# Twelve weight remainders of the first mixer on VectorE instead of in an accumulating DMA, and another order of taking buffers in the second mixer

## The chip, the cores and the metric

The kernel runs on one core of a Trainium2 chip. The metric is the device time of one execution in microseconds (us). All numbers below come from three timed runs of the kernel before and from one profiled execution of it.

## The reference

Two decoder layers over 256 tokens of width 1024 in float32, then a final RMSNorm. Cut to what matters:

```python
x = x + gdn_shortconv_mixer(rms_norm(x), ...)   # layer 0: (256,1024) @ (1024,3600), conv, delta rule, @ (1024,1024)
x = x + squared_relu_mlp(rms_norm(x), ...)      # (256,1024) @ (1024,4096), relu^2, @ (4096,1024)
x = x + nsa_mixer(rms_norm(x), ...)             # layer 1: projections, sparse attention, @ (1024,1024)
x = x + squared_relu_mlp(rms_norm(x), ...)
return rms_norm(x, final_norm)
```

The delta rule of layer 0 works in two chunks per head group: scores of keys against keys, the inverse of a unit lower triangular matrix, then products with values, state and queries. In the kernel the inverse is a ladder of products of 32x32 blocks, in which each step needs the one before it.

## The kernel before, in words

**Weights.** All weights are read once, in pieces of 128 x 1024 float32 (512 KB; the first two pieces of the first layer are smaller, and the compressing weights of layer 1 are used as they are). SyncE's queue issues the loads in order into 8 stage buffers `st`; a load waits until its buffer has been let go (flag `st{slot}`). A piece (a "unit", 204 of them, numbered from 0) isn't used as float32: it is split into a rounded part `uh`, in the type float32r, and the remainder `ul` = `st` - `uh`. A product takes three matmuls: `uh` with the activation's rounded part, `uh` with the activation's remainder, `ul` with the activation's rounded part (`mm256`). A unit of 1024 columns has 8 blocks of 128, so 24 matmuls.

**Who makes the parts.** Two streams run through the units, one through the even numbers and one through the odd (`splits(0)`, `splits(1)`, lines 941 and 942). ScalarE copies `st` into `uh`. There are two ways to `ul`. Normally VectorE subtracts (line 531). For the units that `BYDMA` (line 37) lists, ScalarE first writes -`uh` into `ul`, and then GpSimd issues a DMA that adds `st` onto it (`refill`, line 534). There are four buffers each of `uh` and `ul`; a unit's buffers come free when TensorE has read the unit (flag `ud{i}`). A stage buffer is let go when its unit's `ul` is there (`split_done`), with either way. Units 16 to 35 are projections of the first mixer (four units each for values, queries, and the three parts of the short convolution), 36 to 43 its output projection, 44 to 107 the first MLP, 108 to 139 the second mixer, 140 to 203 the second MLP.

**Who sets the order.** The program is a set of Python generators ("streams"). A planner (`Order`, `run`) holds an estimate of each engine's free time and each instruction's cost, and always lets the stream go on that can start first; ties go to the lower priority number. The order on each engine is fixed in that way when the kernel is built, and on the chip each engine runs its list in order. A stream asks for an engine (`yield 'V'`), for a PSUM bank (`yield BANK`; there are eight), for a flag, or for a token (`yield 'take', name, count`, given back by `give`). The chain of the delta rule has priority 0, the splits 0.5, most else 1 or more; the main stream, which issues the projections, comes last in ties, and fills TensorE between the steps of the chain.

**The chain of the first mixer.** `chain_k` norms the keys, `prepare` forms the key scores `al` and their transposes, `invert` runs the ladder (`tt`, `ys`, `uc` on VectorE, 128 matmuls of 32x32 per step on TensorE), `chain_main` solves for the values, `output` makes `o` and then `ya`, the input of the last four units of the output projection (40 to 43). The query convolution and the short convolution run on GpSimd (`pool_conv`: `tap`, `cvpool`, `CG`).

**The second mixer.** For each of eight head pairs, `attend` makes scores and exponentials `PX`, `weigh` scales them, `combine` spawns four `turn` streams, each of which transposes three 128 x 128 blocks of `PX` on TensorE into a PSUM bank and copies them into one of four buffers `pts`; `products` multiplies them with the values and gives the four `pts` tokens back.

Line 329 is that of a helper that records every compute instruction, so nearly all rows of the profile name it; tiles tell the instructions apart.

Of the kernel before, what the change touches and what calls it, by code (L numbers as in the profile page):

```python
# [33 lines left out]
KPOOL, VPOOL, QPOOL, CVB = (), (), (0, 1, 2, 3), {'conv': 4, 'pool': 2}  # L34
TAP = {'V': 290}
CHAIN, EARLY, TOK_FIRST = 0, 16, False
BYDMA, DLAT = (*range(20, 44, 2), *range(113, 121, 2), *range(129, 141, 2)), 4500
YIELD = (0.0, 0.0, 0.0)
TICK, BUSY = 10240 / 3, 1500.0
FULL, DRAIN, BARE, STAY, LEAVE = (128, 128), 0.0, 0.0, 0.0, 0.0  # L40
# [125 lines left out]
class Order:  # L166
# [21 lines left out]
    def spawn(self, gen, prio=None):  # L188
        c = self.cur
        if prio is None:  # L190
            prio = 1 if c is None or c.prio in (MAIN, SPLIT) else c.prio
        s = Stream(gen, prio, c)
        self.streams.append(s)
        self._next(s, None)

    def flag(self, name):
        self.flags.setdefault(name, self._now())
# [5 lines left out]
    def release(self, bank):  # L203
        self.banks.append((self._now(), self.held.pop(id(bank))[0]))

    def give(self, name):
        self.tokens[name].append(self._now())
# [178 lines left out]
SLOTS, PTS = 4, 4  # L386
# [1179 lines left out]
def layer1(e, n, nxt):  # L1566
# [3 lines left out]
    spawn, flag, release, give = order.spawn, order.flag, order.release, order.give  # L1570
    with ExitStack() as ctx:
# [44 lines left out]
        def copy(dst, src, eng):  # L1616
            n = int(np.prod(src.shape[1:]))
            ps = src.space == PSUM
            pick = yield dict(A=(52 if ps else 95) + 0.83 * n, V=68 + (1.04 if ps else 0.52) * n) if PK else eng
            if pick == 'A':  # L1620
                A.activation(dst, src, AF.Copy)
            else:
                V.tensor_copy(dst, src)
# [157 lines left out]
        def attend(i, p, QQ, use):  # L1781
# [55 lines left out]
            give('qr')  # L1837
            spawn(weigh(i, p, PX, den))
            spawn(combine(i, p, PX))

        def soften(u, s, t, bank, sc, PX, nm, den):
# [98 lines left out]
        def combine(i, p, PX):  # L1940
            u = 2 * i + p
            yield 'flag', f'pw{u}.0'
            if not MERGE:
                ob = yield BANK
                O = ob[:, :T]
            turns, spreads, ts4 = [4], [2], {}
            for b in range(2):
                yield 'flag', f'pw{u}.{b}'
                tss = ts4[b] = [None, None]
                for s in range(2):  # L1950
                    spawn(turn(u, b, s, PX, tss, turns), TURN)
                if not MERGE:
                    spawn(spread(i, p, b, tss, O, spreads))
            if MERGE:
                for b in range(2):
                    for s in range(2):
                        yield 'flag', f'ts{u}.{b}{s}'
                ob = yield BANK
                O = ob[:, :T]
                yield SMALL  # L1960
                for b in range(2):
                    products(p, b, ts4[b], O, not b)
            else:
                yield 'flag', f'pv{u}'
            yield 'flag', 'cmp1'
            yield 'flag', f'pct{i}'
            yield 'PE'
            pct, left = pcts[i]
            if CL:
                x = pct.rearrange("p a t q -> p a (t q)")  # L1970
                e.mm256(O, *VCB2[p], x[:, 0], x[:, 1], False, True)
            else:
                PE.matmul(O, VCB2[p], pct.rearrange("p t q -> p (t q)"), start=False, stop=True)
            left[0] -= 1
            if not left[0]:
                give('pct')
            if ohl[i] is None:
                ohl[i] = p1.tile([128, 2, 2, T], F32R, name=f"ohl{i}", tag=f"ohl{i}")
            yield from hilo(ohl[i][:, 0, p], ohl[i][:, 1, p], O)
            release(ob)  # L1980
            flag(f'o{u}')

        def turn(u, b, s, PX, tss, left):
            tb = yield BANK
            tp = tb[:, :384]
            yield 'take', 'pts', PTS
            yield 'PE'
            e.keep(tb)
            PE.transpose(tp[:, :128], PX[0][:, s, b], ident)
            PE.transpose(tp[:, 128:256], PX[1][:, s, b, :128], ident)  # L1990
            PE.transpose(tp[:, 256:], PX[1][:, s, b, 128:], ident)
            left[0] -= 1
            if not left[0]:
                give(f'slot{u % SLOTS}')
            ts = p2.tile([128, 384], F32, name="pts", tag="pts", bufs=PTS)
            yield from copy(ts, tp, 'V' if s else 'A')
            release(tb)
            tss[s] = ts
            flag(f'ts{u}.{b}{s}')

        def products(p, b, tss, O, first):
            for s in range(2):
                g = 2 * p + s
                PE.matmul(O[64 * s:64 * s + 64], VT[:, 0, b, g * 64:g * 64 + 64], tss[s][:, :256],
                          start=first, stop=False)
            for s in range(2):
                g = 2 * p + s
                PE.matmul(O[64 * s:64 * s + 64, 128:], VT[:, 1, b, g * 64:g * 64 + 64], tss[s][:, 256:],
                          start=False, stop=False)
                give('pts')  # L2010

        def spread(i, p, b, tss, O, left):
            for s in range(2):
                yield 'flag', f'ts{2 * i + p}.{b}{s}'
            yield SMALL
            products(p, b, tss, O, left[0] == 2)
            left[0] -= 1
            if not left[0]:
                flag(f'pv{2 * i + p}')
# [63 lines left out]
```

## Time and profile before

| | |
|---|---|
| three timed runs | 672.41, 672.96, 673.91 us (median 672.96) |
| the profiled execution | 674.54 us, of which the span from first to last instruction is 672.7 us |
| TensorE (PE) | busy 97% of the span, weight loads (PEld) 93%, granted clock 0.988 on the mean |
| VectorE (DVE), ScalarE (ACT), GpSimd (POOL) | busy 68%, 58%, 20% |
| weight loads by SyncE's queue | 107.66 MB, 49.1% of 16 DMA engines' time |
| GpSimd's queue (the accumulating DMAs) | 11.54 MB, 9.0%, 22 issues of 512 KB, 5.4 us from issue to landing |
| instruction fetches (queue q8) | 52 packets of together 0.85 MB |

TensorE is busy nearly all the time, so the table alone doesn't tell what a change in one stage is worth: the stretches, the waits and the granted clock have to be read stage by stage. Times in rows are microseconds from the first instruction; a clock of 1.00 is 2.4 GHz and 0.50 is 1.2 GHz.

### The profile page before, as it was taken

How to read it: one execution, taken by the hardware profiler on the slowest of the kernel's cores; microseconds unless marked ns; L12 is line 12 of the kernel's file. 1: busy time of each engine (PE TensorE's matmuls, PEld its weight loads, DVE VectorE, ACT ScalarE, POOL GpSimd, SP SyncE). 2: the span in 40 equal slices, each digit the busy share in tenths (PEclk: the TensorE clock that was granted, in tenths of full speed). 3: DMA queues.
4: the chain of work that ended last, by engine and by line, in shares of the span. 5: the costliest groups of instructions: out<-in, count | busy, mean ns of one | idle time of the engine just before them, and what ended most of it. 6: DMA issues, size and time to landing. Idle time of an engine off the chain costs nothing.

```text
span 672.7 us, 16231 instructions
## 1 busy us (share of the span) xinstructions
PE 650.2 (97%) x6642; PEld 623.5 (93%) x6644; DVE 460.4 (68%) x899; ACT 387.7 (58%) x727; POOL 134.4 (20%) x179
## 2 busy tenths in 40 slices
PE   8999789999999999999999999999999999999995
PEld 5999679988999999999999886898999999999995
DVE  6998445865887776555566898897678777644441
ACT  7577234445676665434446679898567666434430
POOL 1012765611300000012024352120220000012121
PEclk9999789999999999999999999999999999999999
DMA  8884654556666666666666748653555555555401
GB/s 293 301 211 157 174 147 120 140 150 154 222 186 190 193 192 196 198 193 190 193 189 160 223 158 291 185 128 89 170 206 188 189 195 200 197 191 189 158 1 63
DMA packets 35642, 120.62 MB, mean 179 GB/s; under 512 B 4080, under 2 KB 4592, under 8 KB 35568
## 3 DMA queue, kind: packets, MB, share of 16 engines
q1 hardware_dynamic: 32112, 107.66, 49.1%
q0 software_dynamic: 3168, 11.54, 9.0%
q8 instruction: 52, 0.85, 0.5%
q10 hardware_dynamic: 288, 0.39, 0.2%
q14 instruction: 22, 0.18, 0.1%
HBM read 106.99 MB, written 1.05 MB: 161 GB/s over the span
## 4 chain that ended last, share of the span: by engine, by line
PE 80%; DVE 9%; ACT 4%; issue 3%; DMA 2%; SPq 0%; DVEq 0%; ACTq 0%
PE b L329 80%; DVE ul L329 2%; ACT uh L329 1%; DMA ul<-st 1%; DMA X<-xt 1%; DMA st<-wts 1%; DVE cvconv L329 1%; DVE rqt L329 1%; ACT E L329 1%; ACT ul L329 1%; DVE al L329 1%; DVE lc L329 0%; DVE u L329 0%; DVE tt L329 0%; DVE nacc L329 0%
## 5 line engine op out<-in xcount | busy, mean ns | idle before, releaser
L329 ACT ACTIVATE uh<-st 128x1024 fp32r<-128x1024 f32 (+3 forms) x204 | 206.2, 1012 | 218.4 <-PE b L329 187.5
L329 PE MATMUL b<-x,uh 128*128 128x256 f32 x1664 | 295.6, 282 | 2.0 <-ACT uh L329 1.8
L329 DVE TENSOR_TENSOR ul<-st,uh 128x1024 fp32r<-128x1024 f32 (+3 forms) x182 | 213.9, 1177 | 119.2 <-ACT uh L329 118.9
L329 PEld LDWEIGHTS b<-x,uh 128*128 128x128 f32 x1664 | 254.2, 190 | 4.1 <-ACT uh L329 1.7
L329 PE MATMUL b<-x,ul 128*128 128x256 f32 x832 | 233.1, 280 | 2.5 <-DVE ul L329 1.3
L329 PE MATMUL b<-U,uh 128*128 128x256 f32 x1024 | 174.2, 276 | 0.0
L329 PEld LDWEIGHTS b<-x,ul 128*128 128x128 f32 x832 | 158.2, 190 | 4.0 <-DVE ul L329 2.6
L329 PEld LDWEIGHTS b<-U,uh 128*128 128x128 f32 x1024 | 154.1, 188 | 0.0
L329 PE MATMUL b<-U,ul 128*128 128x256 f32 x512 | 141.3, 276 | 0.0
L329 PEld LDWEIGHTS b<-U,ul 128*128 128x128 f32 x512 | 96.1, 188 | 0.0
L329 POOL TENSOR_TENSOR nacc<-nacc,sq 128x256 f32<-128x256 f32 x24 | 32.4, 1348 | 227.1 <-ACT sq L329 217.4
L329 POOL DMA_DIRECT2D ul<-st x22 | 19.3, 876 | 80.4 <-ACT ul L329 36.4
L329 DVE SCALAR_TENSOR_TENSOR t<-b,rbc 128x256 f32<-128x256 f32 x64 | 26.6, 424 | 8.3 <-PE b L329 8.3
L329 ACT ACTIVATE U<-u 128x256 fp32r<-128x256 f32 x64 | 26.8, 419 | 2.0
L329 ACT ACTIVATE px<-b,nm 128x256 f32<-128x256 f32 (+1 forms) x64 | 26.3, 423 | 2.0 <-DVE nm L329 1.7
L329 DVE TENSOR_TENSOR U<-u,U 128x256 fp32r<-128x256 f32 x64 | 26.5, 419 | 0.0
L329 POOL TENSOR_TENSOR X<-X,par 128x256 f32<-128x256 f32 x8 | 5.6, 702 | 100.3 <-ACT nacc L329 91.7
L329 ACT ACTIVATE u<-t 128x256 f32<-128x256 f32 x64 | 25.6, 401 | 0.0
L329 DVE TENSOR_TENSOR X<-X,b 128x256 f32<-128x256 f32 (+1 forms) x28 | 13.9, 514 | 16.1 <-PE b L329 16.1
L329 PE MATMUL b<-uh,x 128*128 128x264 f32 (+1 forms) x128 | 24.5, 288 | 0.0
L329 PE MATMUL b<-ohl,uh 128*128 128x256 f32 x128 | 23.9, 287 | 0.2
L329 ACT ACTIVATE ul<-uh 128x1024 fp32r<-128x1024 f32 x22 | 23.2, 1057 | 0.4
(276 smaller groups left out, 793.9 us busy)
## 6 DMA issues: line engine op xcount, KB each, us to landing
st<-wts SPq DMA_DIRECT2D x188, 512.0 KB, 4.3
ul<-st POOLq DMA_DIRECT2D x22, 512.0 KB, 5.4
st<-wts SPq DMA_DIRECT2D x8, 280.0 KB, 3.2
st<-wts SPq DMA_DIRECT2D x8, 264.0 KB, 5.9
st<-wts SPq DMA_DIRECT2D x8, 256.0 KB, 6.1
X<-xt SPq DMA_DIRECT2D x3, 256.0 KB, 6.1
par<-par SPq DMA_DIRECT2D x1, 525.0 KB, 5.8
out_dram<-X SPq DMA_DIRECT2D x2, 256.0 KB, 2.7
```

Source lines behind the costliest of these rows:

```text
L329: r = f(*a, **k)
```

## The change

`BYDMA` loses the twelve even units from 20 to 42. Their remainders are made by VectorE's subtraction; ScalarE's writing of -`uh`, GpSimd's DMA issue and the transfer go away for them. The ten units of the second mixer in the list (113 to 119 and 129 to 139, every second one) stay.

In `combine`, the stream of a head pair first takes a token `turns`, of which there is one; it comes back when all four `turn` streams of that pair have taken their `pts` token. And a `turn` takes its `pts` token ahead of its PSUM bank, not after it. The number of buffers, banks and instructions in the second mixer is as before.

```diff
-BYDMA, DLAT = (*range(20, 44, 2), *range(113, 121, 2), *range(129, 141, 2)), 4500
+BYDMA, DLAT = (*range(113, 121, 2), *range(129, 141, 2)), 4500
...
-            turns, spreads, ts4 = [4], [2], {}
+            turns, spreads, ts4 = [4, 4], [2], {}
+            yield 'take', 'turns', 1
...
         def turn(u, b, s, PX, tss, left):
+            yield 'take', 'pts', PTS
+            left[1] -= 1
+            if not left[1]:
+                give('turns')
             tb = yield BANK
             tp = tb[:, :384]
-            yield 'take', 'pts', PTS
             yield 'PE'
             e.keep(tb)
```

## Rows read from the trace of the kernel before

**Rows 1.** Busy time by stretch. Columns: stretch, its length, then busy us (and instructions) of TensorE, of its weight loads, of VectorE, ScalarE and GpSimd, then granted clock, busy share of the DMA engines and GB/s.

```profile
60.00:80.00 20.00, 15.64 (x356) 15.12 (x355) 13.77 (x31) 7.12 (x7) 10.36 (x14) 0.90 0.64 162
80.00:100.00 20.00, 17.08 (x588) 16.00 (x587) 9.41 (x19) 7.51 (x12) 13.69 (x19) 0.84 0.52 129
100.00:120.00 20.00, 20.00 (x485) 19.27 (x485) 11.63 (x29) 8.04 (x12) 11.03 (x17) 0.92 0.45 121
220.00:260.00 40.00, 40.00 (x356) 40.00 (x355) 29.24 (x45) 26.02 (x44) 0.00 (x0) 1.00 0.65 194
```

**Rows 2.** What TensorE waited for from 20 to 190 us: us in total, times, the longest. "issue" is time in which it waited for nothing that the profile shows.

```profile
PE b L329 <- issue: 5.9, 3, 4.1
PE b L329 <- ACT uh L329: 1.1, 1, 1.1
```

**Rows 3.** The timeline of TensorE: the four matmul groups that began after these waits (start, length, instructions, idle time before them).

```profile
76.72 0.49 PE L329 MATMUL b<-ys,uc 32*32 32x32 f32 x21 [4.10 <-issue]
...
86.44 0.34 PE L329 MATMUL b<-ys,uc 32*32 32x32 f32 x18 [0.35 <-issue]
...
94.89 1.25 PE L329 MATMUL b<-ys,uc 32*32 32x32 f32 x122 [1.49 <-issue]
...
98.61 0.37 PE L329 MATMUL b<-x,uh 128*128 128x256 f32 x1 [1.08 <-ACT uh L329]
```

**Rows 4.** DMA packets by queue (packets, MB, share of 16 engines) in four short stretches: 74.3 to 74.5, 83.8 to 84.1, 92.5 to 92.9 and 96.0 to 96.5 us. q8 carries instructions, q0 GpSimd's DMAs, q1 the weight loads; the rows of q8 are shown in that order, after the two data queues of the longer stretch from 62.6 to 74.3 us, in which q8 has no packet.

```profile
q0 software_dynamic: 258, 0.99, 42.7%
q1 hardware_dynamic: 289, 1.05, 34.4%
...
q8 instruction: 1, 0.02, 29.7%
...
q8 instruction: 1, 0.02, 26.3%
...
q8 instruction: 1, 0.02, 15.8%
...
q8 instruction: 1, 0.02, 14.9%
```

**Rows 5.** As rows 4, the data queues from 90 to 98.6 us.

```profile
q0 software_dynamic: 144, 0.52, 31.6%
q1 hardware_dynamic: 201, 0.69, 26.6%
```

**Rows 6.** Stretches cut at the waits and at the changes of the granted clock, columns as in rows 1.

```profile
57.00:72.60 15.60, 15.34 (x317) 14.54 (x317) 14.79 (x38) 6.96 (x8) 5.70 (x7) 1.00 0.57 144
72.60:76.70 4.10, 0.02 (x3) 0.00 (x0) 0.81 (x2) 0.00 (x0) 3.86 (x7) 0.89 0.81 223
76.70:83.00 6.30, 6.28 (x181) 6.00 (x183) 1.38 (x4) 2.42 (x3) 3.43 (x5) 0.53 0.36 98
96.00:103.00 7.00, 5.92 (x43) 5.79 (x30) 2.89 (x6) 2.28 (x5) 0.00 (x0) 0.52 0.50 149
104.00:124.00 20.00, 19.86 (x517) 18.84 (x515) 15.48 (x40) 8.53 (x12) 14.79 (x23) 1.00 0.46 110
```

**Rows 7.** What SyncE's queue, which issues the weight loads, waited for most from 20 to 190 us.

```profile
SPq L482 <- DMA ul<-st: 88.1, 12, 11.4
```

**Rows 8.** Groups of instructions from 36 to 174 us: engine, operation, tiles, count, busy us, mean ns, idle time before.

```profile
L329 DVE TENSOR_TENSOR ul<-st,uh 128x1024 fp32r<-128x1024 f32 x16 | 20.2, 1266 | 9.1 <-ACT uh L329 9.1
L329 ACT ACTIVATE ul<-uh 128x1024 fp32r<-128x1024 f32 x12 | 12.7, 1059 | 0.4
L329 POOL DMA_DIRECT2D ul<-st x12 | 10.6, 880 | 43.8 <-ACT lsq L329 20.6 <-ACT ul L329 14.6 <-ACT eg L329 5.8
```

**Rows 9.** The timelines of ScalarE and VectorE: first the two writings of -`uh` between 57 and 72.6 us, then the step `ys` of the chain's ladder.

```profile
60.82 1.06 ACT L329 ACTIVATE ul<-uh 128x1024 fp32r<-128x1024 f32 x1
...
66.26 1.06 ACT L329 ACTIVATE ul<-uh 128x1024 fp32r<-128x1024 f32 x1
...
69.84 1.52 DVE L329 TENSOR_TENSOR ul<-st,uh 128x1024 fp32r<-128x1024 f32 x1
71.28 0.74 DVE L329 TENSOR_TENSOR ys<-b,par 128x256 f32<-128x256 f32 x2
```

**Rows 10.** The chain's end: ScalarE's timeline, and the last waits of TensorE ahead of `ya`'s matmuls.

```profile
152.71 1.06 ACT L329 ACTIVATE ul<-uh 128x1024 fp32r<-128x1024 f32 x1
153.67 0.61 ACT L329 ACTIVATE osq<-o 128x512 f32<-128x512 f32 x1
...
161.42 0.38 PE L329 MATMUL b<-ya,uh 128*128 128x256 f32 x1 [0.69 <-ACT ya L329]
...
162.15 0.39 PE L329 MATMUL b<-ya,uh 128*128 128x256 f32 x1 [0.34 <-DVE ya L329]
```

**Rows 11.** GpSimd and VectorE side by side: a convolution step of GpSimd alone, a subtraction of VectorE, and the same step of GpSimd while that subtraction ran.

```profile
83.72 0.61 POOL L329 TENSOR_TENSOR cvpool<-prepool,par 128x256 f32<-128x256 f32 x1
...
85.93 1.43 DVE L329 TENSOR_TENSOR ul<-st,uh 128x1024 fp32r<-128x1024 f32 x1 [0.57 <-ACT uh L329]
86.23 1.60 POOL L329 TENSOR_TENSOR cvpool<-prepool,par 128x256 f32<-128x256 f32 x1
```

**Rows 12.** The attention of the second mixer: a stretch as in rows 1, and the largest wait of TensorE from 360 to 490 us.

```profile
400.00:420.00 20.00, 19.59 (x166) 13.13 (x165) 17.27 (x45) 18.07 (x58) 6.70 (x13) 1.00 0.74 239
...
PE b L329 <- DMA ul<-st: 1.1, 1, 1.1
```

## The prediction, made before the result was known

> **What bounds the kernel now.** I read the stretches first. In the MLP TensorE is busy in every microsecond at full clock, 356 matmuls in 40 us [rows 1]; there an edit of VectorE's or a DMA's work buys nothing. The first mixer is where the change works (units 20 to 42, from about 38 to 160 us), and it has the one weak stretch of the kernel: from 60 to 100 us TensorE is idle for 4.36 + 2.92 us, and from 60 to 120 us its granted clock is 0.84 to 0.92 on the mean [rows 1]. So I read the waits of that part. The largest isn't for an engine: 5.9 us of "issue" in three waits, then 1.1 us put down to ScalarE's `uh` [rows 2]. The timeline places them: 4.10, 0.35, 1.49 and 1.08 us, together 7.02 us, three of them in the middle of a group of 32x32 matmuls [rows 3].
>
> What released them is seen in the DMA queues. Just ahead of each of the four, the instruction queue q8 moved one 16 KB packet (first seen in the stretches from 74.3, 83.8, 92.5 and 96.0 us), and TensorE went on 2.4 to 2.6 us after the start of those stretches. Before the longest wait no such packet had moved from 62.6 to 74.3 us, while GpSimd's queue took 42.7% and the weight loads 34.4% of the sixteen engines [rows 4]. I read this as: the ladder's short matmuls use up instructions faster than anywhere else (317 matmuls from 57 to 72.6 us [rows 6] against 356 in 40 us), TensorE runs out of them, and the next packet is late because data transfers are ahead of it. That also covers the fourth wait, since the `uh` it is put down to ended only because TensorE itself had come late.
>
> The clock follows the gaps: 0.53 from 76.7 to 83 us, after the longest, and 0.52 from 96 to 103 us, after the third [rows 6]; both are stretches at 1.2 GHz but for their edges. From 104 to 124 us there are as many short matmuls, TensorE is busy for 19.86 of 20 us, and the clock is 1.00 [rows 6]: the ladder alone doesn't lower it.
>
> The Trainium skill says otherwise of the first point ("Runtime: NRT & Kernel Launch", section "Instruction fetch mechanics"): instructions are refilled in blocks of 16 KiB over a DMA queue of their own, and crossing a block costs little because it is mostly hidden. The packet size agrees with rows 4, the hiding doesn't in these four places. What the kernel would do if the waits weren't due to the refill is a rival below.
>
> **The change, part by part.** The sum is made against the profiled execution, 674.54 us (span 672.7 us and 1.84 us around it); the median of the runs shown is 1.58 us lower, and the forecast is moved by that.
>
> *Transfers that go away.* Twelve accumulating transfers of 512 KB leave. In the worst stretch they were 42.7 of 77.1 parts of the traffic (55%), from 90 to 98.6 us 31.6 of 58.2 (54%) [rows 4, 5]. They also bunch the weight loads: SyncE's queue waits 88.1 us in twelve waits for these transfers before it may refill a stage buffer [rows 7], and the odd unit behind is then ready too, so two loads go out back to back. With VectorE's subtraction the buffers come free one by one. I scale each wait by the traffic left: 4.10 x 0.45 = 1.8, 1.49 and 1.08 x 0.46 = 1.2, and 0.35 to 0, since only q0 was busy in that spot. 3.0 us stay, 4.0 us go. Bounds: 0 and 7.0 us.
>
> *Clock.* The two slow stretches cost half their TensorE work: 6.28 x (1 - 0.53) = 3.0 us and 5.92 x (1 - 0.52) = 2.8 us, together 5.8 us. Without the long gap I expect no first drop; the second is less sure, since two shorter gaps made it. I take 4.5 us; bounds 0 and 5.8 us.
>
> *VectorE.* Twelve subtractions come in; sixteen in the same stretch took 1.266 us each [rows 8], so 12 x 1.266 = 15.2 us of work. ScalarE loses 12 x 1.059 = 12.7 us, GpSimd 12 x 0.88 = 10.6 us [rows 8]. VectorE's work lies beside TensorE's where the chain isn't late, so only what delays the chain counts. From 57 to 72.6 us VectorE is busy for 14.79 of 15.60 us and carries the chain into the ladder [rows 6]; two of the units fall there (their -`uh` at 60.82 and 66.26 us), and how such a subtraction sits in front of a step is seen at 69.84 us, where `ys` follows at once [rows 9]. That is 2 x 1.266 = 2.5 us in full. The other ten meet a VectorE that is idle about 30 to 50% of the time [rows 1]; a chain step comes every few microseconds, and I take a fifteenth part of each as delay, 10 x 1.266 / 15 = 0.8 us, an estimate. At the end the chain gains: `osq` starts right behind a writing of -`uh` (152.71 to 153.67 us), so it can start 1.0 us earlier, but a subtraction comes in on VectorE in the same place; I count 0.3 us of gain. Sum: 3.0 us later. It counts in full, because the chain's end is already what TensorE waits for: 0.69 + 0.34 us ahead of `ya`'s matmuls [rows 10]. Bounds: -1.0 us (only `osq`'s gain) and 15.2 us (all twelve on the chain).
>
> What is queued behind the new subtraction: on VectorE the chain's steps and the evacuations of banks. The subtraction itself waits for ScalarE's `uh`, as VectorE's sixteen do now, for 9.1 us in all [rows 8]; twelve more of these waits are in the 3.0 us as far as they hit the chain.
>
> *GpSimd.* Its in-order list loses the waits for -`uh`, 14.6 us [rows 8], and the issues. I cost this at nothing, since TensorE's list of waits doesn't name GpSimd; bounds -1 and 1 us. The Trainium skill has a rule against the change here ("SBUF — State Buffer", the part on the port pair that VectorE and GpSimd share): a VectorE operation with two SBUF inputs and a GpSimd operation that reads SBUF shut each other out for the whole instruction. The trace agrees: a convolution step of 0.61 us takes 1.60 us beside a subtraction [rows 11]. By the rule each new subtraction that meets one costs GpSimd 1.0 us, about what the lost issue gives back, so the sum stays.
>
> *Second mixer.* TensorE is idle for 0.41 of 20 us from 400 to 420 us, and its largest wait there is 1.1 us for an accumulating transfer that stays [rows 12]. Taking `pts` ahead of the bank frees banks for scores, and the token `turns` can hold back the next head pair's transposes, which would wait for `pts` anyway. I take 0; bounds -1 and 2 us, a shift of the planner's order included.
>
> Sum: -4.0 - 4.5 + 3.0 = -5.5 us, so 669.0 us for a profiled execution and 667.5 us for the median. The likeliest case's own range is 663 to 671 us.
>
> **The rivals.** *All gaps go, the clock stays up and the chain is hidden:* -7.0 - 5.8 = -12.8 us, 660.2 us. For it: the bunched loads go with the transfers. Against: weight loads alone still hold up refills. *It evens out:* the waits shrink by 4.0 us, both slow stretches stay, the chain costs 3.0 us: 672.0 us; for it, the ladder's short matmuls stay what they are. *VectorE becomes the bound (slower):* the place is the run from 57 us through the ladder to the solves at 104 to 124 us, where VectorE is busy for 15.48 of 20 us [rows 6]; the price is 1.266 us for every subtraction that stands ahead of a chain step. It decides from the seventh on, where 7 x 1.266 = 8.9 us exceeds the 8.5 us of gain; with nine, 672.96 - 8.5 + 11.4 = 675.9 us. For it: both ends of the chain are without slack. Against: the planner lets the chain go first in a tie. *The gaps have another cause and stay:* only the 3.0 us count, 676.0 us; this is what the skill's rule on refills amounts to. Against it stand the four packets. *The change doesn't do what it says* can only hold for its second part (0 us, in the sum already).
>
> **How the numbers follow.** Forecast 0.50, everything hidden 0.13, evens out 0.15, VectorE the bound 0.12, another cause 0.10. A difference under 0.2% (1.35 us) can't be told from no change for this kernel, so "same" is 671.6 to 674.3 us. Of the forecast 0.48 lies below, 0.02 within; of "evens out" 0.05 below and 0.10 within; all of the first rival is faster, and nearly all of the last two slower. Faster 0.66, same 0.13, slower 0.21. The range must reach to both sides: 661 us leaves out about half of the first rival, 675.5 us a bit over half of the last two.
>
> **What would show it.** Right: no packet on q0 before about 360 us; no gap of over 2 us on "issue" between 55 and 105 us and at most one stretch at 1.2 GHz there; SyncE's queue no longer waiting for `ul<-st`; the matmuls on `ya` beginning some 5 us before 161.4 us, with TensorE's wait ahead of them longer than 1.0 us by the chain's delay. Wrong: the same gaps at the same q8 packets without q0 in the way (then weights alone starve the refill), a wait for `ya` of 6 us or more (VectorE bound), or a difference that arises after 360 us.

## The result and the profile after

The changed kernel takes 666.62 us (median of four runs, 665.16 to 667.17); the kernel before, run beside it on the same chip, takes 673.43 us. The medians differ by 6.8 us. The ratio estimated from the single runs is 0.9883, with a 95% interval of 0.9845 to 0.9922, so by the ratio it is 7.9 us (5.2 to 10.4). 667.5 us had been forecast. The profiled execution took 666.40 us with a span of 664.6 us, 8.1 us shorter than before; the accounts below are made against that.

Where the span became shorter is read from the times at which the same matmuls start on TensorE in both traces (us; the last column is worked out from unrounded times):

| TensorE | before | after | difference |
|---|---|---|---|
| first matmul of the ladder (`tt,al`) | 68.57 | 68.53 | 0.0 |
| last matmul of the ladder (`ys,uc`) | 120.47 | 111.01 | -9.5 |
| first matmul on `ya` | 161.42 | 154.25 | -7.2 |
| last matmul on `ya`,`uh` | 172.84 | 164.90 | -7.9 |
| last matmul of the first MLP on `U`,`uh` | 348.6 | 340.6 | -7.9 |
| first matmul of the second MLP on `U`,`uh` | 575.5 | 567.0 | -8.5 |

The gain is made in one place, the ladder, which takes 42.5 us where it took 51.9. Not all of these 9.5 us are saved, for 26 fewer matmuls lie in it (the ladder from its first matmul to its last, before and after, columns as in [rows 1]):

```profile
68.57:120.66 52.09, 44.81 (x1376) 42.55 (x1375) 27.17 (x62) 17.36 (x25) 34.00 (x49) 0.87 0.56 147
...
68.53:111.20 42.67, 39.09 (x1350) 36.84 (x1349) 33.02 (x65) 11.89 (x20) 34.03 (x44) 0.96 0.37 112
```

From there to the first matmul on `ya` it is 2.3 us more than before. Of these, 2.0 us are work that came over from the ladder (447 matmuls in 41.15 busy us, where there were 425 in 39.16), and 0.3 us are waits. `ya`'s own matmuls bring 0.8 us, and the rest of the kernel runs as before to within 0.6 us.

The stretches answer to [rows 1, 6], columns as there:

```profile
60.00:80.00 20.00, 18.90 (x513) 18.29 (x513) 18.72 (x37) 4.85 (x6) 7.83 (x11) 1.00 0.51 161
80.00:100.00 20.00, 17.52 (x595) 16.05 (x594) 13.04 (x23) 5.69 (x9) 18.39 (x24) 0.91 0.31 87
100.00:120.00 20.00, 19.07 (x419) 18.09 (x418) 17.40 (x42) 7.01 (x13) 12.19 (x18) 1.00 0.32 101
...
90.00:93.00 3.00, 1.22 (x53) 1.06 (x41) 1.27 (x4) 0.42 (x1) 2.77 (x6) 1.00 0.63 182
93.00:96.80 3.80, 3.80 (x98) 3.58 (x100) 2.23 (x6) 1.23 (x2) 2.89 (x5) 0.55 0.03 10
```

From 60 to 80 us TensorE now does 513 matmuls where it did 356, at full clock. One short stretch at 1.2 GHz is left (0.55 from 93.0 to 96.8 us, its edges included), where there were two [rows 6]. It too stands right behind a gap: from 90 to 93 us TensorE is busy for 1.22 us only.

TensorE's waits from 20 to 190 us, and the two groups that began after "issue", answer to [rows 2, 3]:

```profile
PE b L329 <- issue: 2.2, 2, 1.8
PE b L329 <- DVE ys L329: 1.4, 2, 1.1
PE b L329 <- DVE u L329: 0.9, 2, 0.7
PE b L329 <- DVE yb L329: 0.6, 1, 0.6
```

```profile
88.46 0.39 PE L329 MATMUL b<-x,ul 128*128 128x256 f32 x1 [0.43 <-issue]
...
92.19 0.25 PE L329 MATMUL b<-ys,uc 32*32 32x32 f32 x4 [1.78 <-issue]
```

The four waits of together 7.0 us have become two of 2.2 us. In their place stand small waits for VectorE, 2.9 us in all, of which hardly any were there before (the rows of before that [rows 2] doesn't show):

```profile
PE b L329 <- DVE o L329: 0.7, 2, 0.4
PE b L329 <- ACT ya L329: 0.7, 1, 0.7
PE b L329 <- ACT Vf L329: 0.7, 1, 0.7
...
PE b L329 <- DVE ya L329: 0.3, 1, 0.3
PE b L329 <- DVE ys L329: 0.3, 1, 0.3
```

Just ahead of the wait of 1.78 us the DMA queues from 89.0 to 90.3 us show what moved beside the instruction packet; this answers to [rows 4]:

```profile
q1 hardware_dynamic: 108, 0.39, 73.8%
q8 instruction: 1, 0.02, 5.0%
```

GpSimd's queue is empty here, and the weight loads alone fill 73.8% of the sixteen engines. That they are what keeps this wait isn't shown: e5 below has the same wait almost without loads.

SyncE's queue has a new first wait, which answers to [rows 7]; the subtractions of the same stretch answer to [rows 8]:

```profile
SPq L482 <- DVE ul L329: 58.2, 22, 7.7
```

```profile
L329 DVE TENSOR_TENSOR ul<-st,uh 128x1024 fp32r<-128x1024 f32 x33 | 42.5, 1295 | 9.2 <-ACT uh L329 9.1
```

### The profile page after: what moved, and what is told of

Read it like the earlier page. It is cut to its first block, busy times and chain, and to the rows that moved or that the text cites. A ratio compares the mean times of both kernels' runs of the same rounds, so it can differ in the third digit from the quotient of the medians.

```text
span 664.6 us, 16204 instructions
## 1 busy us (share of the span) xinstructions
PE 646.4 (97%) x6642; PEld 621.1 (93%) x6644; DVE 474.0 (71%) x911; ACT 375.4 (56%) x715; POOL 127.5 (19%) x167
## 3 DMA queue, kind: packets, MB, share of 16 engines
q0 software_dynamic: 1440, 5.24, 4.1%
## 4 chain that ended last, share of the span: by engine, by line
PE 83%; DVE 9%; ACT 2%; issue 2%; DMA 2%; SPq 0%; POOLq 0%; DVEq 0%; ACTq 0%
PE b L329 83%; DVE ul L329 3%; DVE cvconv L329 2%; ACT uh L329 1%; DMA X<-xt 1%; DMA ul<-st 1%; DVE rqt L329 1%; DVE al L329 1%; DVE lc L329 1%; ACT ul L329 0%; DVE preconv L329 0%; SPq L482 0%; DVE r L329 0%; DVE kst L329 0%; DVE tt L329 0%
## 5 line engine op out<-in xcount | busy, mean ns | idle before, releaser
L329 DVE TENSOR_TENSOR ul<-st,uh 128x1024 fp32r<-128x1024 f32 (+3 forms) x194 | 229.5, 1185 | 118.0 <-ACT uh L329 117.5
L329 PEld LDWEIGHTS b<-uh,x 128*128 128x128 f32 x128 | 20.3, 188 | 0.2 <-issue 0.2
L329 PEld LDWEIGHTS b<-ohl,uh 128*128 128x128 f32 x128 | 19.6, 188 | 0.7 <-ACT ohl L329 0.3
```

What stands on the lines that cost most here:

```text
L329: r = f(*a, **k)
```

## The experiments

All ratios are against the kernel before, run on the same chip. "Issue" is TensorE's wait of that name from 20 to 190 us, beside 5.9 us before (and 1.1 us of the same kind put down to `uh`) and 2.2 us after.

**Which part of the change?** Part one alone (e1) is the kernel before with

```diff
-BYDMA, DLAT = (*range(20, 44, 2), *range(113, 121, 2), *range(129, 141, 2)), 4500
+BYDMA, DLAT = (*range(113, 121, 2), *range(129, 141, 2)), 4500
```

> Only the first part of the change: the twelve units' remainders by VectorE, with the transposes taking their buffers as before. My theory: all of the gain is in the first mixer and comes from this part; 666.5 us (664.5 to 668.5), within 1.5 us of the changed kernel. Rival (the second part brings a share, by banks freed in the second mixer): 668 us or more, with the difference arising after 360 us.

Measured: 666.73 us, ratio 0.9898 (0.9866 to 0.9929), issue 2.8 us in two waits, the longest 2.3. Part two alone (e2) is the changed kernel with the same line turned round.

> Only the second part of the change: the twelve transfers stay. My theory: 673.4 us like the kernel before (672 to 675), the four gaps at the ladder and both stretches at 1.2 GHz as before. Rival (the second part brings a share): 671 us or less.

Measured: 674.28 us, ratio 1.0009 (0.9990 to 1.0029), and the long gap is back (issue 5.4 us in two waits, the longest 4.1). All of the gain is part one's. Part two moves nothing: set side by side, with and without it the instruction lists of all engines are the same but for serial numbers in the names of some buffers, which lie at the same addresses. So e1 is the changed kernel executed again, and e2 the kernel before: what differs between the traces of such a pair differs from execution to execution.

**Traffic or order?** With part one, the planner also puts every engine's instructions in another order. To keep the order of before, this kernel (e3) keeps every instruction and every flag and only makes the twelve transfers narrow (TensorE's list gets three waits for semaphores more by it, and the remainders are left out in the other columns).

```diff
-        G.dma_start(lo.bitcast(F32), src, accum_op=OP.add)
+        w = 32 if i < 44 else UN
+        G.dma_start(lo[:, :w].bitcast(F32), src[:, :w], accum_op=OP.add)
```

> The kernel before with its instruction order on every engine, but the twelve accumulating transfers move 32 of 1024 columns each (16 KB for 512 KB), so that the remainders of these units are left wrong in the other columns: only the traffic goes, and the time for which it holds the stage buffers. Theory (instruction fetches are late because data transfers are in the way): the 'issue' waits from 60 to 100 us fall from 5.9 us to 3 us or less, at most one short stretch at 1.2 GHz stays, and the time falls to 663 to 668 us, as no subtraction comes in on VectorE. Rival (the gain comes from the planner's new order, not from the traffic): the waits stay above 5 us and the time stays at 672 to 674 us.

Measured: 668.02 us, ratio 0.9925 (0.9900 to 0.9951). The wait list has five waits of up to 1.4 us, where one was 4.1 us long; their sum is more than the 3 us that had been expected:

```profile
PE b L329 <- issue: 4.2, 5, 1.4
```

The stretch from 60 to 120 us, first of this kernel and then of the kernel before:

```profile
60.00:120.00 60.00, 55.49 (x1530) 52.59 (x1529) 41.27 (x96) 25.90 (x34) 42.22 (x60) 1.00 0.36 102
```

```profile
60.00:120.00 60.00, 52.73 (x1425) 50.38 (x1425) 34.82 (x79) 22.66 (x30) 35.08 (x50) 0.89 0.54 137
```

In the same order, with the traffic gone (DMA share 0.36 for 0.54), 5.0 us of the change's 7.9 come by the ratios, 4.8 of 6.8 by the medians. The clock stays at 1.00 although 4.2 us of short waits remain. The gain doesn't need the new order; whether the order has a share in the rest, the intervals don't tell.

**The traffic, or that it holds the stage buffers?** The prediction named both. In the next kernel (e8) the transfer reads `uh` in place of `st` (so the remainder comes out as zero), and a stage buffer no longer waits for it.

```diff
-                spawn(refill(i, lo[:, :n], src), SPLIT)
+                spawn(refill(i, lo[:, :n], hi[:, :n].bitcast(F32) if i < 44 else src), SPLIT)
```

> The kernel before with the twelve accumulating transfers at full size, in the same order, but reading the rounded part and not the stage buffer: the same kind and amount of traffic, while the stage buffer is let go as soon as ScalarE has read it (the remainders of twelve units become zero). If the transfers' own traffic makes the fetches late: 671 to 674 us, with waits on issue of 5 us or more from 60 to 100 us. If the hold on the stage buffers does it, by bunching the weight loads: 666 to 669 us, as with the thin transfers (668.0 us).

Measured: 672.92 us, ratio 0.9981 (0.9956 to 1.0005). SyncE's first wait, TensorE's wait and the stretch from 60 to 120 us, each from its view:

```profile
SPq L482 <- DVE ul L329: 73.5, 19, 11.8
```

```profile
PE b L329 <- issue: 7.8, 6, 4.1
```

```profile
60.00:120.00 60.00, 51.97 (x1461) 49.47 (x1461) 36.82 (x85) 22.18 (x29) 37.97 (x54) 0.94 0.60 152
```

No load waits for a transfer any more, and the gaps are as long as before. It is the transfers' own packets that hold up the refill, not the moment at which they let the buffers go.

**Is it the refill at all?** If the gaps come when a packet of instructions is used up, their place depends on how many instructions TensorE has executed, and on nothing in the program's sense. So 64 tiny matmuls were put at the very start of the kernel before (e7).

```diff
+        for _ in range(64):
+            nc.tensor.matmul(b[:32, :32], w[:32, :32], w[:32, :32], start=True, stop=True)
```

> The kernel before with 64 more tiny matmuls (128 instructions with their weight loads, half of a 16 KB packet of instructions) on zeros at the very start, in the same order else. Theory (the gaps are TensorE running out of instructions, so their places are set by a count of instructions from the start): the first long gap, which came after 79 of the 128 matmuls of the ladder's first ys,uc group, comes 64 matmuls earlier in the program, after some 15 of that group; the one after 6 of 128 in the third ys,uc group moves back into the tt,al group before it, after some 85 of 128. Rival (a wait of these matmuls themselves, for a buffer or a semaphore that the profile doesn't show): the gaps stay after 79 and after 6.

One execution was timed, 675.61 us, so the time says little; the trace is what counts. TensorE's `ys,uc` groups of 128 matmuls that a gap cut in two, 71 to 98 us, first of the kernel before and then of this one:

```profile
71.75 0.87 PE L329 MATMUL b<-ys,uc 32*32 32x32 f32 x79 [0.26 <-DVE ys L329]
76.72 0.87 PE L329 MATMUL b<-ys,uc 32*32 32x32 f32 x49 [4.10 <-issue]
85.53 0.57 PE L329 MATMUL b<-ys,uc 32*32 32x32 f32 x43
...
93.14 0.26 PE L329 MATMUL b<-ys,uc 32*32 32x32 f32 x6
```

```profile
71.19 0.32 PE L329 MATMUL b<-ys,uc 32*32 32x32 f32 x15 [0.26 <-DVE ys L329]
75.03 1.72 PE L329 MATMUL b<-ys,uc 32*32 32x32 f32 x113 [3.52 <-issue]
84.41 1.13 PE L329 MATMUL b<-ys,uc 32*32 32x32 f32 x107
87.69 0.38 PE L329 MATMUL b<-ys,uc 32*32 32x32 f32 x21 [2.15 <-issue]
95.40 0.80 PE L329 MATMUL b<-ys,uc 32*32 32x32 f32 x70
96.79 0.69 PE L329 MATMUL b<-ys,uc 32*32 32x32 f32 x58 [0.58 <-issue]
```

The cuts stood after 79, 43 and 6 matmuls. They now stand after 15, 107 and 70: 79 - 64 = 15, 43 - 64 + 128 = 107, 6 - 64 + 128 = 70. The third was expected in the `tt,al` group before, after some 85; that group has no cut. Counted from the start of the trace, the first long gap comes after the same number of matmuls in both kernels (the stretch up to it, before and in this run):

```profile
0.00:72.65 72.65, 68.14 (x730) 62.11 (x731) 62.55 (x163) 47.05 (x93) 13.45 (x24) 1.00 0.77 239
...
0.00:73.00 73.00, 68.52 (x730) 62.90 (x731) 62.48 (x162) 47.30 (x93) 13.57 (x25) 1.00 0.78 241
```

In the kernel before, 256, 255 and 128 recorded matmuls lie between one of the four waits and the next, the one put down to `uh` included (a record can be missing). A wait of these matmuls themselves, for data or a semaphore, would have stayed where it was in the program. The places repeat every 128 matmuls, each with its weight load, so 256 instructions, which is one packet of q8. The Trainium skill gives the same number ("Runtime: NRT & Kernel Launch", section "Instruction fetch mechanics": blocks of 16 KiB, 256 instructions); that the cost of a block's end is mostly hidden doesn't hold in this ladder.

**Traffic put back (e4).** The changed kernel, with a copy of 512 KB by GpSimd's queue beside each of the twelve subtractions, to a place that nothing reads.

```diff
+                if 20 <= i < 44 and i % 2 == 0:
+                    nc.gpsimd.dma_start(spare[(i - 20) // 2], bass.AP(tensor=wts.tensor, offset=wts.offset + pieces[p][0], ap=[[UN, 128], [1, UN]]))
```

> The changed kernel with its instruction order, and beside each of the twelve subtractions a transfer of 512 KB from the weights to an unused DRAM tensor, issued by GpSimd, on which nothing waits: only traffic comes back, without its hold on the stage buffers. Theory (traffic delays the instruction fetches): the 'issue' waits in the ladder rise from 2.2 us to 4 us or more, a full stretch at 1.2 GHz comes back, and the time rises by 3 to 8 us to 669.5 to 674.5 us. Rival (planner's order): 666 to 668 us, waits as in the changed kernel.

Measured: 669.25 us, ratio 0.9943 (0.9915 to 0.9972); issue 2.6 us in one wait. The time is just under what was expected, the wait well under. The copies aren't like the transfers that they stand for: over the whole run GpSimd's queue shows 1824 packets where the changed kernel has 1440, so 384 for twelve copies, and they go out at other moments. The interval overlaps the changed kernel's, and the profiled execution (666.80 us) is the fastest of the six, so the trace doesn't show where the time went. It speaks for a cost of traffic and settles nothing by itself.

**What does VectorE's new work cost?** Once it was taken away and once doubled, in the order of the changed kernel: the twelve subtractions cover 32 of 1024 columns, with TensorE reading `uh` in the place of `ul`, while the planner is charged in full (e5), or each is done twice (e6).

```diff
-                V.tensor_sub(lo[:, :n], src, hi[:, :n].bitcast(F32))
+                if 20 <= i < 44 and i % 2 == 0:
+                    made[i] = hi, hi
+                    nc.vector.tensor_sub(lo[:, :32], src[:, :32], hi[:, :32].bitcast(F32))
+                    order.spend('V', *V.cost('tensor_sub', (lo[:, :n], src, hi[:, :n].bitcast(F32)), {}))
+                else:
+                    V.tensor_sub(lo[:, :n], src, hi[:, :n].bitcast(F32))
```

> The changed kernel with its instruction order on TensorE, but the twelve subtractions cover 32 of 1024 columns, and TensorE reads these units' rounded part in the place of the remainder (the remainders of twelve units are left out). It takes VectorE's new work away. Theory of the prediction (the subtractions delay the chain by 3.0 us): 663.6 us (662 to 665.5). Rival (VectorE's new work is hidden): 666 to 667.5 us, within 1 us of the changed kernel.

```diff
+                if 20 <= i < 44 and i % 2 == 0:
+                    nc.vector.tensor_sub(lo[:, :n], src, hi[:, :n].bitcast(F32))
                 V.tensor_sub(lo[:, :n], src, hi[:, :n].bitcast(F32))
```

> The changed kernel with each of the twelve subtractions made twice, unknown to the planner, so in the same order: another 12 x 1.2 = 14.6 us on VectorE in the same places. Theory of the prediction (a fifth of this work stands ahead of the chain): 3 us more, 669 to 671 us, or somewhat over, as slack is used up. Rival (hidden): at most 1 us more. Rival (VectorE is the bound already): 8 us more or above, 674 us.

Without the work: 668.12 us, ratio 0.9891 (0.9849 to 0.9933), not shown to be faster than the changed kernel. By themselves the two intervals leave room for the 3.0 us of the prediction, so the traces have to decide. The delay that the run was to remove is real. In the changed kernel VectorE does two subtractions between the ladder's `uc` and its `ys`, and TensorE waits for `ys` (the timelines of VectorE and TensorE):

```profile
68.36 0.45 DVE L329 STREAM_TRANSPOSE uc<-tt 128x256 f32<-128x256 f32 x1
68.73 2.32 DVE L329 TENSOR_TENSOR ul<-st,uh 128x1024 fp32r<-128x1024 f32 x2
...
72.08 0.74 DVE L329 TENSOR_TENSOR ys<-b,par 128x256 f32<-128x256 f32 x2
```

```profile
72.56 0.64 PE L329 MATMUL b<-ys,uc 32*32 32x32 f32 x51 [1.10 <-DVE ys L329]
```

Only one of the two is new: in e5 one of 1.22 us is still there. Without the new work the ladder begins 1.24 us earlier (67.29 us) and this group 2.45 us earlier, and it runs dry (timeline, wait list and stretch of this run):

```profile
70.11 0.85 PE L329 MATMUL b<-ys,uc 32*32 32x32 f32 x76
73.57 0.95 PE L329 MATMUL b<-ys,uc 32*32 32x32 f32 x52 [2.61 <-issue]
```

```profile
PE b L329 <- issue: 5.5, 4, 2.6
```

```profile
60.00:80.00 20.00, 17.39 (x441) 16.59 (x442) 14.11 (x31) 4.77 (x6) 7.91 (x12) 0.83 0.55 160
```

What the earlier `ys` won, the next wait for instructions took, and the clock fell behind it (0.83 from 60 to 80 us). The last matmul on `ya`,`uh` starts at 165.04 us, beside 164.90 in the changed kernel. Since the stage buffers also come free earlier in e5, the loads come at other moments; how much of the 2.61 us is due to them wasn't separated.

This run shows one thing more. Its wait of 1.80 us stands at the same matmul as the changed kernel's 1.78 us, after 124 of a `ys,uc` group, but here the data queues are almost empty ahead of it (TensorE's timeline, and the queues from 91.2 to 93.1 us):

```profile
91.15 0.72 PE L329 MATMUL b<-x,uh 128*128 128x256 f32 x4 [0.98 <-issue]
...
94.88 0.25 PE L329 MATMUL b<-ys,uc 32*32 32x32 f32 x4 [1.80 <-issue]
```

```profile
q8 instruction: 1, 0.02, 3.8%
q1 hardware_dynamic: 3, 0.01, 1.1%
```

From the end of one wait for instructions to the end of the next, 128 matmuls on, it is 94.88 - 91.15 = 3.73 us, of which TensorE works for 1.93. In the changed kernel it is 92.19 - 88.46 = 3.73 us too, with loads on 73.8% of the engines. So a refill that followed the one before took 3.7 us even without data in its way, longer than 128 mostly short matmuls last, and this part of the waits needs no traffic.

With the work done twice: 679.08 us, ratio 1.0073 (1.0045 to 1.0101), so 12.5 us over the changed kernel for some 15 us of work. Its list of TensorE's waits:

```profile
PE b L329 <- DVE ys L329: 4.2, 2, 2.9
...
PE b L329 <- DVE u L329: 2.6, 2, 2.3
```

That is over the 3 us that were expected, in the range of the rival by which VectorE is the bound. The first 15 us of VectorE's work cost nothing that shows at the end of `ya`, the next 15 us nearly their full price.

**Is there more to be had?** Four more versions of the changed kernel: the second mixer's ten units by subtraction too (e9); the ladder as two streams of 64 matmuls per step, one for each chunk (e10); and the even units 36 to 42 (e11), or 20, 22 and 36 to 42 (e12), back by transfer.

```diff
-BYDMA, DLAT = (*range(113, 121, 2), *range(129, 141, 2)), 4500
+BYDMA, DLAT = (), 4500
```

> The changed kernel with an empty list: the ten units of the second mixer are subtracted on VectorE too. In the second mixer TensorE never gaps on issue (its matmuls are long), so the reason that paid in the first mixer is missing there, and VectorE is busy for 19.2 of 20 us from 380 to 400 us. Theory: no gain, 666 to 669 us, with what the one wait for a transfer (0.7 us) gives back. Rival (any transfer less is a gain): 664.5 us or less.

Measured: 672.31 us, ratio 0.9969 (0.9949 to 0.9989), 5.7 us slower than the changed kernel where a gain or nothing was expected. From the last matmul on `U`,`uh` of the first MLP to the first of the second it is 575.6 - 341.8 = 233.8 us, and 567.0 - 340.6 = 226.4 us in the changed kernel. A stretch of the second mixer, first of the changed kernel and then of this one:

```profile
380.00:400.00 20.00, 19.88 (x151) 16.46 (x149) 19.20 (x46) 17.13 (x61) 9.33 (x19) 1.00 0.55 189
```

```profile
380.00:400.00 20.00, 17.61 (x118) 14.42 (x120) 19.02 (x47) 12.56 (x45) 8.82 (x19) 1.00 0.34 116
```

VectorE is full there in both, and with the subtractions on it TensorE and ScalarE get less done. The kind of transfer that costs in the ladder pays here.

```diff
-                for c in range(2):
-                    al, tt, _, _ = parts[c]
-                    for h in range(8):
...
+            yield 'flag', f'parts{c}'
+            al, tt, uc, ys = parts[c]
```

> The changed kernel with the ladder as two streams, one per chunk, of 64 short matmuls a step in place of 128 for both: the same instructions, in bursts half as long, and one chunk's VectorE steps beside the other's matmuls. If the ladder's pace is set by the steps' latency, it gets shorter and the time falls to 663 to 665.5 us. If it is set by how fast instructions come in, the waits on issue stay at 2 us or more and the time stays at 666 to 668 us.

Measured: 670.17 us, ratio 0.9936 (0.9918 to 0.9955), in neither theory's favour: the ladder begins 9.0 us earlier (59.54 us) and its last `ys,uc` starts 8.6 us later (119.6 us) than in the changed kernel; issue 4.1 us in three waits. Why it takes that long wasn't settled.

```diff
+BYDMA, DLAT = (*range(36, 44, 2), *range(113, 121, 2), *range(129, 141, 2)), 4500
```

> The changed kernel with the four units behind the ladder (36, 38, 40, 42) by accumulating transfer again, the eight up to 34 by VectorE. Theory (transfers cost where the short matmuls run, VectorE costs where the chain runs without them): from the ladder's last matmul to the first on ya the kernel before took 41.0 us and the changed one 43.2 us, so 1 to 2 us are to be had: 664.5 to 666 us. Rival (a transfer less is a gain anywhere in the first mixer): 667.5 us or more.

Measured: 665.29 us, ratio 0.9885 (0.9834 to 0.9935). In the trace the part from the ladder's end to the first matmul on `ya` is 41.75 us, 1.5 us shorter than in the changed kernel, as expected (TensorE's idle time in it falls from 1.9 to 0.95 us); the ratio is the changed kernel's own, so it isn't shown to be faster.

```diff
+BYDMA, DLAT = (20, 22, *range(36, 44, 2), *range(113, 121, 2), *range(129, 141, 2)), 4500
```

> As the run before, and units 20 and 22, whose transfers end before the ladder begins, by transfer too. Theory: they relieve VectorE where it is busy for 19 of 20 us (40 to 60 us), but the ladder's pace is set by how fast instructions come, so no more than 1 us: 664 to 666 us. Rival (VectorE sets the start of the ladder and so the end): 663 us or less.

Measured: 667.74 us, ratio 0.9915 (0.9886 to 0.9943), above both ranges. The relief of VectorE ahead of the ladder didn't bring it forward: the planner put the steps in another order, and the wait for `ys` is 2.4 us. No version was shown to beat the changed kernel.

## Why the prediction was right, and where it wasn't

**What bounds the kernel: right.** The ladder's short matmuls run out of instructions because the next packet is late. Three runs carry this: the places of the gaps move by exactly the 64 matmuls put in, modulo 128 (e7); in an unchanged order the waits shorten when the transfers get thin (e3), and they don't when the transfers stay and only their hold on the buffers goes (e8). The rival "another cause" falls with them. What the prediction didn't have is that the packet can be late without any data ahead of it (e5).

**Transfers that go away: right in size, wrong in one reason.** Forecast -4.0 us, measured 7.0 - 2.2 = -4.8 us. That each wait scales with the traffic left came near in sum, not one by one: the longest went away altogether, and a wait of 1.78 us stayed near 92 us, as long as e5's with empty queues. That the size came out is luck in that respect: the 3.0 us that were to stay had been put down to the weight loads. The step that "they also bunch the weight loads", and that with the subtraction "the buffers come free one by one", failed. Without the hold the gaps stay (e8), and in the changed kernel the loads still fill 73.8% of the engines at one time.

**Clock: right.** Forecast -4.5 us of the 5.8 us lost; now (1 - 0.55) x 3.80 = 1.7 us are lost, so -4.1 us in this pair of traces. It is not a fixed part of the kernel: e1, the same instructions, has the gap at 2.33 us and no loss in the ladder (80 to 100 us of that run):

```profile
80.00:100.00 20.00, 17.09 (x681) 15.80 (x682) 13.09 (x23) 6.21 (x10) 18.73 (x24) 1.00 0.34 98
```

In the kernels before and after each stretch at 1.2 GHz in the ladder stands behind a gap, and the five short ones of e3 brought none.

**VectorE: the work right, its price wrong.** This is the step that failed. The prediction set 2 x 1.266 = 2.5 us ahead of `ys`, and taking the work away brings `ys,uc` forward by 2.45 us (e5). Against the kernel before, though, the ladder begins as early as it did (68.53 for 68.57 us) and that group only 0.81 us later (72.56 for 71.75). And "it counts in full, because the chain's end is already what TensorE waits for" doesn't hold: the wait ahead of `ya` was one of its kind, while inside the ladder a group of short matmuls that begins earlier runs dry sooner (e5). The first matmul on `ya` (154.25 us) now follows the one before it without a wait. On TensorE's list the term is what came new, less what went: `ys`, `u` and `yb` have 2.9 us now where `ys` had 0.3; 1.0 us for `ya`, 0.7 for `Vf` and some 0.5 for `o` are gone. That is about +0.4 us, not +3.0. The sum of the three terms, -4.8 - 4.1 + 0.4 = -8.5 us, stands beside the 7.9 us by which the first mixer became shorter. At the chain's end a gain of 0.3 us had been counted for `osq`; with units 36 to 42 back by transfer that part is 1.5 us shorter (e11), so there the subtractions were a loss. "VectorE becomes the bound" has its place and price right but decides later: twelve subtractions stay below the point, twenty-four are far beyond it (e6).

**GpSimd: right.** Five of its convolution steps from 74 to 98 us now take 1.6 us, as [rows 11] had it for one. TensorE's list names GpSimd no more than before.

**Second mixer: right.** Forecast 0; the part from MLP to MLP became 0.6 us shorter, and part two changes no instruction (e2). Its largest wait stays the kind that it was, `ul` by transfer, now of 0.7 us.

**The number.** 667.5 us came within 0.9 us of the result, which is in part luck. The sum was -5.5 us; between the two profiled executions it is -8.1 us, and most of the difference is VectorE's term. The medians moved by 6.8 us.

**Of what was to show it,** there is no wait of over 2 us, one stretch at 1.2 GHz, no wait of SyncE for the transfers, and `ya` came 7.2 us earlier rather than 5. That the wait ahead of `ya` would be longer than 1.0 us was wrong: there is none. "All gaps go" (660.2 us) is refuted by the 2.2 us that stay.

## What to carry to other kernels

A burst of many short matmuls is fed by instruction packets that share the DMA engines with the data, so in such a stretch a wait on "issue" in the middle of a group, with a q8 packet just ahead of it, says: look at the DMA queues, and move transfers elsewhere, even at the price of work on another engine. Part of the wait can stay with empty queues: here a packet's 128 matmuls lasted 1.9 us, and the next packet came into use 3.7 us after the one before. Whether a wait is of this kind is told by shifting the count of instructions, and by thinning the transfers in an unchanged order; a change that also reorders the program can't tell it. Price an engine's added work by what TensorE would do with the time, not by the delay itself: here the first 15 us showed no cost in the sum and the next 15 us cost 12.5, and the same transfer that hurt in the ladder paid where VectorE was full.

## What was not expected of the hardware

The gaps stand at a fixed count of TensorE's instructions, to the single matmul (79 to 15, 43 to 107, 6 to 70 after 64 more). A group that began 2.45 us earlier lost all of that lead to the next wait for instructions (2.61 us). A refill takes 3.7 us with the data queues almost empty, where 128 mostly short matmuls last 1.9. And the length of a gap alone doesn't tell whether the clock falls: behind the 1.78 us of the changed kernel it did (0.55), behind e1's 2.33 us, in the same instructions, it didn't, and behind this one of e8 it stayed at 1.00 from 75 to 80 us:

```profile
74.12 0.62 PE L329 MATMUL b<-ys,uc 32*32 32x32 f32 x49 [2.37 <-issue]
```

What decides between the two was not tried. Nor is it known why the changed kernel's profile has a granted clock of 0.57 from 11 to 15 us, where e1, executing the same instructions, has 1.00; the ladder begins at the same time as before, so it has no part in the result.
